# Moving a mixture-of-experts overflow branch into the expert loop, and three modulation chunks behind three projections

## The chip, the cores and the metric

The kernel runs on one core of a Trainium2 chip. The metric is the time of one execution on the device, in microseconds. The kernel before takes 1628.29 us (median of 3 runs, 1628.29 to 1628.72). The engines are TensorE (PE in the rows, its weight loads PEld), VectorE (DVE), ScalarE (ACT), GpSimd (POOL) and SyncE (SP); a letter q behind an engine's name stands for its sequencer, which takes branches, semaphores and the issue of transfers.

## The reference

Two layers over 256 latent and 256 context tokens of width 1024. Each layer normalises and modulates the tokens, projects them once, runs three token mixers (grouped-query attention, neighbourhood attention, an mLSTM scan) and merges them; then comes a mixture of experts. The modulation vectors come from a product with `w_mod` of each layer.

```
for l in range(DEPTH):                         # DEPTH = 2
    mod = silu(c) @ w_mod[l] + b_mod[l]        # and mod_c of the context vector: shifts, scales, gates
    h = modulate(rms_norm(x, g_norm[l, 0]), sh1, sc1)
    y, yc = token_mixers(h, hc, ...)           # h @ w_in, three branches, merge
    x = x + gt1 * y
    h = modulate(rms_norm(x, g_norm[l, 1]), sh2, sc2)
    x = x + gt2 * hier_moe(h, ...)
    # in layer 0 the same for the context tokens xc

def hier_moe(t):                               # top-1 of 4 groups, top-2 of its 8 experts
    for e in range(32):
        gu = t @ w_gate_up[e]
        y = (silu(gu[:, :256]) * gu[:, 256:]) @ w_down[e]
        out = out + dense_w[:, e:e+1] * y      # dense_w is 0 for the experts not chosen
```

In layer 0 the mixture of experts runs over 512 tokens (two halves of 256), in layer 1 over the 256 latent tokens.

## The kernel before

The tokens stand transposed, features on the 128 partitions, as eight tiles of 128 features (`KT` = 8). The kernel is recorded as straight code for five engines; a scheduler that plans over a time line orders the instructions of each engine, but it moves none across the edge of a block. A branch (`tc.If`) begins and ends a block, so nothing recorded behind it can be put ahead of it.

**The experts (`moe`).** Each expert has room for 32 tokens (`CAP`) of a half. The loop `for q in range(NQ)` takes four experts at a time, eight times. `gather` collects the tokens of experts by matmuls with one-hot matrices (L1270), `gate_up(q)` does the first product (L1309), `swiglu` the activation, `act_T(q)` turns the result (L1329), `down` does the second product (L1344), and `combine(q)` scatters the rows back by matmuls (L1234) and adds them to the tokens with VectorE (L1239). TensorE runs `gate_up(q)` ahead of `down(q-1)`. The weights come by SyncE, 1 MB to a transfer (L1026, `in_wgu` and `in_wdn`), into buffers that are free again when TensorE has used them; `fetch_up(l, q+2)` and `fetch_down(l, q+1)` issue them ahead.

**The overflow path (L1397 to L1453).** Behind the loop every engine loads the largest rank of a token within an expert (`mi`, TENSOR_LOAD of L1397) and compares it (L1399). Only if an expert has more than 32 tokens of a half, a loop over all experts computes the tokens left out; its weights come by SyncE into the `wraw` buffers. With these inputs the path is not taken: the trace has no instruction of its body. An engine that jumps the body first raises the semaphores that the body would have raised, and before it does, it waits for what it has under way itself; on SyncE these are its transfers. The branch stands once in each layer.

**The layer boundary.** Ahead of the branch in layer 0 stand the first weight of layer 1's projections (`prep(T["win"][1, 12])`) and two modulation chunks. `mod_chunk` multiplies 256 columns of `w_mod` (L238), turns the result (L243) and adds the bias. Behind the branch `mixers(1)` issues three `w_mod` transfers into `y` buffers (`held`, L707). The first projection (`pre_w`, of tokens scaled by their gain only, L370 and L371, in two parts h0 and l0) doesn't need the norm of the tokens; it is scaled afterwards (L700). Then come six modulation chunks (the three held ones and those of `mod_fill(2)`), the projections `win[13]`, `win[10]`, `win[11]`, and `winp`. Those need the normalised tokens: L286 and L301 on TensorE, L290, L323, L330 and L380 on VectorE. Each projection's weights are split into a high and a low part by ScalarE (L221) and VectorE (L222), and each product is three matmuls (L334, L335, L336).

Of the kernel before, what the change touches and what calls it, by code (L numbers as in the profile page):

```python
# [10 lines left out]
F32 = mybir.dt.float32  # L11
# [34 lines left out]
def tile_backbone(ctx: ExitStack, tc: tile.TileContext, T, out):  # L46
# [310 lines left out]
    def mixers(l, need_ctx, xsrc, stats):  # L357
# [351 lines left out]
        for c in range(2):  # L709
            if c < len(pre_w):  # L710
                proj_f(pre_w[c], N, lambda i, p: use_k(2 * c + i, p, True), h0, l0)
                for m, w in held:
                    mod_chunk(*m, pat, w)
                if held:
                    mod_fill(2)
                held = []
            else:
                proj_f(win[12 + c], N, lambda i, p: use_k(2 * c + i, p, False))
        for c in range(2):
            proj_f(win[10 + c], nq, lambda i, p: nc.scalar.copy(qTM[:, 2 * c + i, :nq], p))  # L720
        for f in shares:
# [398 lines left out]
    def moe(l, nt, st, rt):  # L1120
# [227 lines left out]


# [12 lines left out]
        for q in range(NQ):  # L1362
# [4 lines left out]
            if q > 0:  # L1367
                aT = act_T(q - 1)
# [11 lines left out]
            if o < 3:  # L1380
# [4 lines left out]
                if q % 2 == 1:  # L1385
                    xe = xe_next
        down(NQ - 1, act_T(NQ - 1))
        combine(NQ - 1)
        if l == 0:
            lead.append((prep(T["win"][1, 12]), norm_scale(1, 0, slice(0, KT))))  # L1390
            for _ in range(2):
# [4 lines left out]

        top = nc.values_load(mi[0:1, 0:1], min_val=0, max_val=2048,  # L1397
                             skip_runtime_bounds_check_because="the key is 1024 + a rank below 512, or a rank")
        with tc.If(top >= 1024 + CAP):  # L1399
            over = t2([512])[:, :ntt * 32].rearrange("p (t e) -> p t e", e=32)  # L1400
            nc.vector.tensor_scalar(over, key, float(1024 + CAP), None, op0=ALU.is_ge)
            nc.vector.tensor_tensor(out=dw[:, :ntt], in0=dw[:, :ntt], in1=over, op=ALU.mult)
            ec = mt[:, 512:544]
            nc.vector.tensor_copy(ec, iota32)
            hT = Slabs([s8("mg", [4, N]) for _ in range(2)], 4)
            for t in range(ntt):
                for k in range(KT):
                    q = ptr()
                    c = slice(128 * k, 128 * k + 128)
                    nc.tensor.matmul(q[:, :128], lhsT=hth[t // 2][:, t % 2, c].bitcast(F32), rhs=ident, start=True, stop=False)  # L1410
                    nc.tensor.matmul(q[:, :128], lhsT=htl[t // 2][:, t % 2, c].bitcast(F32), rhs=ident, start=False, stop=True)
                    nc.vector.tensor_scalar(
                        hT[k][:, 128 * t:128 * t + 128], q[:, :128], modT[l][:, 24 + k, t // 2:t // 2 + 1], None, op0=ALU.add)
            with tc.For_i(0, NQ, 1) as q4:
                for e in range(4):
                    g0, g1 = (wraw(
                        T["wgu"][l, bass.ds(q4, 1), 4 * hf:4 * hf + 4, :, e].rearrange("o k p n -> p (o k) n"), [4, 512])
                        for hf in range(2))
                    w0 = wraw(T["wdn"][l, bass.ds(q4, 1), :, :, :, e].rearrange("o c k p n -> p (o c k) n"), [4, 512])
                    wq = small([32])  # L1420
                    nc.vector.tensor_scalar(wq, ec, 0.0, 0.5, op0=ALU.is_equal, op1=ALU.mult)
                    nc.vector.tensor_scalar(ec, ec, -1.0, None, op0=ALU.add)
                    pickd = t2([512])[:, :ntt * 32].rearrange("p (t e) -> p t e", e=32)
                    nc.vector.tensor_tensor(
                        out=pickd, in0=dw[:, :ntt], in1=wq.unsqueeze(1).to_broadcast([128, ntt, 32]), op=ALU.mult)
                    wt = small([ntt])
# [147 lines left out]
```

## Time and profile before

| | |
|---|---|
| median of the runs | 1628.29 us (1628.29 to 1628.72) |
| the profiled execution, its span | 1630.45 us, 1628.7 us |
| TensorE | 1520.8 us busy, 93% |
| weight loads of TensorE | 1055.9 us, beside it |
| VectorE, ScalarE, GpSimd | 777.7, 593.2, 168.8 us |
| read from HBM | 344.33 MB, 213 GB/s over the span |
| expert loop of layer 0, from gate_up(0) to the last output matmul | 709.1 to 969.9 us |
| pause of SyncE's issues at the layer boundary | 947.43 to 976.56 us |
| expert loop of layer 1 | 1413.4 to the end |

The page's share of TensorE is a mean over stages with different limits; where the change acts, windows and timelines of single engines are read. Idle time of an engine is followed by what ended it, in brackets. [...]

### The profile page before, as it was taken

The numbers are of one execution on the slowest core, as the hardware profiler recorded it, in microseconds if no ns is written. First come the engines' busy times: TensorE is split into PE (matmuls) and PEld (weight loads), VectorE is DVE, ScalarE is ACT, GpSimd is POOL, SyncE is SP. The second block draws the span as 40 slices with busy tenths as digits, with TensorE's granted clock in tenths as the row PEclk, the third lists the DMA queues.
The fourth block names the chain that finished last, engine by engine and source line by source line (L and its number), as shares of the span: only waits on it lengthen the run. The fifth ranks groups of instructions, "written<-read, shape, count | busy, mean of one in ns | idle before, by whom it ended". The sixth has DMA issues, their size and how long they took to land. (4 is left out here: it accounts for less than half of the span.)

```text
span 1628.7 us, 26090 instructions
## 1 busy us (share of the span) xinstructions
PE 1520.8 (93%) x10713; PEld 1055.9 (65%) x10713; DVE 777.7 (48%) x1754; ACT 593.2 (36%) x1195; POOL 168.8 (10%) x154
## 2 busy tenths in 40 slices
PE   5999999999999999979999978999999999797776
PEld 3688789767767678844434435989978789632221
DVE  4637953543345425253334357378556556431222
ACT  4325642443343333432122135346355455311110
POOL 2200320100021003000000002003011112000000
PEclk9999999999999999989999998999999999898898
DMA  8552234323322154258999968642225448699998
GB/s 305 183 176 83 104 111 156 116 70 114 134 98 84 40 176 152 80 219 350 405 385 413 390 267 312 208 137 78 91 104 169 149 146 324 251 417 417 416 418 328
DMA packets 57200, 349.27 MB, mean 214 GB/s; under 512 B 6912, under 2 KB 8032, under 8 KB 20336
## 3 DMA queue, kind: packets, MB, share of 16 engines
q1 hardware_dynamic: 54720, 341.02, 54.7%
q10 hardware_dynamic: 1616, 5.24, 0.8%
q0 software_dynamic: 736, 1.24, 0.4%
q8 instruction: 88, 1.44, 0.4%
q14 instruction: 40, 0.33, 0.1%
HBM read 344.33 MB, written 3.15 MB: 213 GB/s over the span
## 5 line engine op out<-in xcount | busy, mean ns | idle before, releaser
L222 DVE TENSOR_TENSOR wlo<-wraw,whi 128x1024 fp32r<-128x1024 f32 (+1 forms) x152 | 191.6, 1262 | 173.4 <-ACT whi L221 157.4
L334 PE MATMUL mm<-h,whi 128*128 128x512 f32 (+1 forms) x656 | 227.1, 348 | 0.5 <-ACT whi L221 0.5
L335 PE MATMUL mm<-h,whi 128*128 128x512 f32 (+1 forms) x656 | 223.4, 342 | 0.0
L336 PE MATMUL mm<-h,wlo 128*128 128x512 f32 (+1 forms) x656 | 222.4, 343 | 0.1
L221 ACT CAST whi<-wraw 128x1024 fp32r<-128x1024 f32 (+1 forms) x152 | 155.5, 1026 | 170.7 <-PE mm L335 68.1
L334 PE MATMUL mm<-whi,h 128*128 128x256 f32 (+1 forms) x640 | 183.0, 289 | 0.0
L336 PE MATMUL mm<-whi,h 128*128 128x256 f32 (+1 forms) x640 | 182.8, 288 | 0.0
L335 PE MATMUL mm<-wlo,h 128*128 128x256 f32 (+1 forms) x640 | 182.2, 286 | 0.0
L334 PEld LDWEIGHTS mm<-h,whi 128*128 128x128 f32 x656 | 123.8, 189 | 35.7 <-issue 17.5
L336 PEld LDWEIGHTS mm<-h,wlo 128*128 128x128 f32 x656 | 123.4, 189 | 23.3 <-issue 10.1
L335 PEld LDWEIGHTS mm<-h,whi 128*128 128x128 f32 x656 | 124.2, 190 | 17.0 <-issue 5.3
L334 PEld LDWEIGHTS mm<-whi,h 128*128 128x128 f32 x640 | 121.5, 191 | 6.6 <-issue 4.0
L335 PEld LDWEIGHTS mm<-wlo,h 128*128 128x128 f32 x640 | 122.1, 191 | 1.0 <-DVE G L775 0.5
L336 PEld LDWEIGHTS mm<-whi,h 128*128 128x128 f32 x640 | 121.6, 191 | 1.5 <-issue 1.4
L1309 PE MATMUL at<-qkv,y 128*32 128x512 f32 x792 | 104.9, 615 | 8.1 <-DMA qkv<-in_wgu 8.0
L1239 DVE SCALAR_TENSOR_TENSOR qkv<-mm,c_modT,qkv 128x256 f32<-128x256 f32 x192 | 80.5, 477 | 38.6 <-PE mm L1234 38.6
L619 DVE TENSOR_REDUCE nmx<-at 128x1 f32<-128x512 f32 (+1 forms) x96 | 56.7, 599 | 54.7 <-PE at L605 53.9
L1309 PE MATMUL at<-wraw,y 128*32 128x512 f32 x552 | 74.5, 625 | 8.9 <-DMA wraw<-in_wgu 8.9
L537 POOL TENSOR_TENSOR s1p<-s1p,c_powm 128x8 f32<-128x8 f32 (+1 forms) x24 | 43.4, 1807 | 315.5 <-DVE s1p L535 114.0
L1317 DVE SCALAR_TENSOR_TENSOR a<-a,at 128x256 f32<-128x256 f32 x24 | 10.1, 421 | 136.8 <-ACT a L1316 136.8
L1275 ACT ACTIVATE y<-mm,c_modT 128x256 f32<-128x256 f32 x96 | 40.2, 471 | 94.0 <-PE mm L1270 91.7
L1316 ACT ACTIVATE a<-at 128x256 f32<-128x256 f32 x24 | 9.2, 384 | 178.5 <-PE at L1309 178.0
(378 smaller groups left out, 2586.9 us busy)
## 6 DMA issues: line engine op xcount, KB each, us to landing
qkv<-in_wgu SPq DMA_DIRECT2D x62, 1024.0 KB, 11.8
wraw<-in_win SPq DMA_DIRECT2D x56, 1024.0 KB, 4.8
wraw<-in_wgu SPq DMA_DIRECT2D x42, 1024.0 KB, 11.6
wraw<-in_wmod SPq DMA_DIRECT2D x39, 1024.0 KB, 4.9
qkv<-in_wdn SPq DMA_DIRECT2D x31, 1024.0 KB, 9.6
wraw<-in_wdn SPq DMA_DIRECT2D x19, 1024.0 KB, 11.8
h<-in_wgu SPq DMA_DIRECT2D x14, 1024.0 KB, 17.5
wraw<-in_wbr SPq DMA_DIRECT2D x24, 512.0 KB, 3.3
```

Source lines behind the costliest of these rows:

```text
L221: nc.scalar.copy(hv, src)
L222: nc.vector.tensor_sub(lv, src, hv.bitcast(F32))
L334: nc.tensor.matmul(out_, lhsT=lh, rhs=rh, start=first, stop=False)
L335: nc.tensor.matmul(out_, lhsT=lh, rhs=rl, start=False, stop=False)
L336: nc.tensor.matmul(out_, lhsT=ll, rhs=rh, start=False, stop=last)
L537: nc.gpsimd.tensor_tensor(out=r, in0=v, in1=powm[:, :2 * H], op=ALU.pow)
L619: nc.vector.tensor_reduce(nmx[:, hf:hf + 1], S[hf], axis=AX.X, op=ALU.max, negate=True)
L1239: nc.vector.scalar_tensor_tensor(xT[f][:, c], p[:, c], modT[l][:, 40 + f, v_:v_ + 1], xT[f][:, c], op0=ALU.mult, op1=ALU.add)
L1275: nc.scalar.activation(xe[:, k], p[:, 256 * (k % 2):256 * (k % 2) + 256], AF.Identity, bias=modT[l][:, 24 + k, v_:v_ + 1])
L1309: nc.tensor.matmul(gps[v_][CAP * e:CAP * e + CAP], lhsT=xe[v_][:, k, s0:s0 + CAP], rhs=w[e], start=(k == 0), stop=(k == KT - 1))
L1316: nc.scalar.activation(th[:, 0:256], gp[:, 0:256], AF.Tanh, bias=0.0, scale=0.5)
L1317: nc.vector.scalar_tensor_tensor(th[:, 0:256], th[:, 0:256], 1.0, gp[:, 0:256], op0=ALU.add, op1=ALU.mult)
```

## The change

Three things are changed.

- In `moe` the overflow path becomes a function, `overflow()`, called once in each layer's loop behind `q == 0`, with `act_T(0)` ahead of it. It thus stands ahead of `gate_up(1)`, `down(0)` and `combine(0)`.
- Its body takes its weights by GpSimd's queue into tiles of the `a2` pool, one 128 x 512 piece for each product, and turns the tokens anew for each expert. The statistics that it computed anew at its end are gone, since the tokens are complete only after the loop.
- In `mixers(1)` the three held chunks and `mod_fill(2)` stand behind `win[13]`, `win[10]` and `win[11]`.

```
             if c < len(pre_w):
                 proj_f(pre_w[c], N, lambda i, p: use_k(2 * c + i, p, True), h0, l0)
-                for m, w in held:
-                    mod_chunk(*m, pat, w)
-                if held:
-                    mod_fill(2)
-                held = []
             else:
                 proj_f(win[12 + c], N, lambda i, p: use_k(2 * c + i, p, False))
         for c in range(2):
             proj_f(win[10 + c], nq, lambda i, p: nc.scalar.copy(qTM[:, 2 * c + i, :nq], p))
+        for m, w in held:
+            mod_chunk(*m, pat, w)
+        mod_fill(2 if held else 0)
...
+        def overflow():
+            top = nc.values_load(mi[0:1, 0:1], min_val=0, max_val=2048, ...)
+            with tc.If(top >= 1024 + CAP):
...
+                def weights(src):
+                    w = a2([512])
+                    nc.gpsimd.dma_start(w, src.rearrange("o p n -> p (o n)"))
+                    return w
+                with tc.For_i(0, NQ, 1) as q4:
...
             if q > 0:
-                aT = act_T(q - 1)
+                if q > 1:
+                    aT = act_T(q - 1)
                 gps = [pat() for _ in range(ns)]
                 gate_up(q, xe, gps)
...
                 if q % 2 == 1:
                     xe = xe_next
+            if q == 0:
+                aT = act_T(0)
+                overflow()
         down(NQ - 1, act_T(NQ - 1))
         combine(NQ - 1)
...
-        top = nc.values_load(mi[0:1, 0:1], min_val=0, max_val=2048, ...)
-        with tc.If(top >= 1024 + CAP):
...
-                    g0, g1 = (wraw(T["wgu"][l, bass.ds(q4, 1), 4 * hf:4 * hf + 4, :, e]...) for hf in range(2))
-                    w0 = wraw(T["wdn"][l, bass.ds(q4, 1), :, :, :, e]...)
...
-            if nxt[0] is not None:
-                nxt[0].n = 0
-                for f in range(KT):
-                    nxt[0].step(xT[f])
-            else:
-                for f in range(0, KT, 2):
-                    emit(f)
```

What the scheduler makes of it, at three places. The first is TensorE in layer 0's loop, before: the last gathers (L1270), the turning of the activated rows of the first four experts (L1329) and their successors' first product (L1309, on the weights `qkv_6084` and on).

```order
2973 L1270 MATMUL mm_6495<-whi_6413,h_6175 128x256
2974 L1270 MATMUL mm_6495<-whi_6413,h_6176 128x256
2975 L1329 MATMUL tr_6506<-c_ident,a_1144_6418 128x128 x2
2976 L1309 MATMUL at_6513<-qkv_6084,y_6246 32x512
2977 L1329 MATMUL tr_6506<-c_ident,a_1145_6422 128x128 x2
2978 L1309 MATMUL at_6513<-qkv_6084,y_6246 32x512 x3
2979 L1309 MATMUL at_6514<-qkv_6084,y_6247 32x512 x4
2980 L1309 MATMUL at_6513<-qkv_6086,y_6246 32x512 x4
```

And with the change, up to the branch (its lines are now L1268, L1327 and L1307; L1349 and L1351 are the load and the compare; L1289 is a helper product for the next scatter):

```order
2975 L1268 MATMUL mm_6495<-whi_6413,h_6176 128x256
2976 L1327 MATMUL tr_6506<-c_ident,a_1144_6418 128x128 x2
2977 L1327 MATMUL tr_6506<-c_ident,a_1145_6422 128x128 x2
2978 L1289 MATMUL ao_8592<-rwT_6167,t_1853_8589 128x512
2979 L1349 TENSOR_LOAD mi_6173
2980 L1351 COMPARE_AND_BRANCH
```

The jump lands ahead of the first product of the next four experts:

```order
3642 L1363 UNCONDITIONAL_BRANCH
3643 L1351 UNCONDITIONAL_BRANCH
3644 L1307 MATMUL at_8389<-qkv_6084,y_6246 32x512 x4
3645 L1307 MATMUL at_8390<-qkv_6084,y_6247 32x512 x4
3646 L1307 MATMUL at_8389<-qkv_6086,y_6246 32x512 x4
```

Before, the first product began between the two halves of act_T(0); now both halves, a helper product and the branch stand ahead of it, and the body of the branch (672 matmuls in layer 0, 288 before) lies between.

The second place is SyncE at the layer boundary, before: the last two weights of the experts (`in_wdn`), the first weight of layer 1 (`in_win`), the branch, the three held transfers into `y` and those that follow it (the rows of the body lie between this piece and the next).

```order
191 L1026 DMA qkv_7916<-in_wdn 128x2048
192 L1026 DMA wraw_7918<-in_wdn 128x2048
193 L204 DMA wraw_8348<-in_win 128x2048
194 L1397 TENSOR_LOAD mi_6173
195 L1399 COMPARE_AND_BRANCH
```

SyncE behind the branch's body, before:

```order
226 L1399 UNCONDITIONAL_BRANCH x2
227 L707 DMA y_9218<-in_wmod 128x2048
228 L707 DMA y_9220<-in_wmod 128x2048
229 L707 DMA y_9222<-in_wmod 128x2048
230 L204 DMA wraw_9276<-in_wmod 128x2048
231 L204 DMA wraw_9338<-in_wmod 128x2048
232 L204 DMA wraw_9355<-in_wmod 128x2048
233 L204 DMA wraw_9372<-in_win 128x2048
```

SyncE with the change, at the same place:

```order
200 L1024 DMA qkv_9792<-in_wdn 128x2048
201 L707 DMA y_10430<-in_wmod 128x2048
202 L707 DMA y_10432<-in_wmod 128x2048
203 L1024 DMA wraw_9794<-in_wdn 128x2048
204 L204 DMA wraw_10224<-in_win 128x2048
205 L204 DMA wraw_10488<-in_wmod 128x2048
206 L707 DMA y_10434<-in_wmod 128x2048
207 L204 DMA wraw_10505<-in_win 128x2048
208 L204 DMA wraw_10567<-in_wmod 128x2048
209 L204 DMA wraw_10584<-in_win 128x2048
```

No branch stands there any more: two held transfers go ahead of the last `in_wdn`, the third follows closely, and the weight of `win[13]` (`wraw_10505`) is the third transfer behind the lead weight, with `wraw_10584` (of `win[10]`) two behind it.

The third place is VectorE at the layer boundary, before: the end of the sums of squares (L277), the branch, L371, and the normalised tokens from L323 on.

```order
1076 L277 TENSOR_TENSOR acc_8269<-acc_8269,a_1613_9053 128x512
1077 L277 TENSOR_TENSOR acc_8269<-acc_8269,a_1614_9056 128x512
1078 L1399 UNCONDITIONAL_BRANCH x2
1079 L290 TENSOR_SCALAR s1p_9110<-ao_9105 128x4
1080 L371 SCALAR_TENSOR_TENSOR qkv_9068<-qkv_5610,smp_8358,qkv_9066 128x256 x8
1081 L371 SCALAR_TENSOR_TENSOR qkv_9069<-qkv_5611,smp_8358,qkv_9067 128x256 x8
1082 L323 TENSOR_TENSOR a_1633_9148<-qkv_5610,acc_9119 128x512
1083 L323 TENSOR_TENSOR a_1637_9162<-qkv_5610,acc_9119 128x512
1084 L330 TENSOR_SCALAR t_1632_9147<-a_1633_9148,smp_8358,c_modT_129 128x256
1085 L330 TENSOR_SCALAR t_1634_9154<-a_1635_9155,smp_8358,c_modT_129 128x256
```

VectorE with the change, at the same place:

```order
1270 L371 SCALAR_TENSOR_TENSOR qkv_10281<-qkv_5611,smp_10234,qkv_10279 128x256 x4
1271 L408 TENSOR_REDUCE shb_10277<-at_10333 128x4
1272 L371 SCALAR_TENSOR_TENSOR qkv_10281<-qkv_5611,smp_10234,qkv_10279 128x256 x2
1273 L277 TENSOR_TENSOR acc_10145<-acc_10145,a_2103_10211 128x512
1274 L371 SCALAR_TENSOR_TENSOR qkv_10281<-qkv_5611,smp_10234,qkv_10279 128x256
1275 L222 TENSOR_TENSOR wlo_10508<-wraw_10505,whi_10507 128x1024
1276 L277 TENSOR_TENSOR acc_10145<-acc_10145,a_2105_10221 128x512
1277 L222 TENSOR_TENSOR wlo_10512<-wraw_10505,whi_10511 128x1024
1278 L290 TENSOR_SCALAR s1p_10322<-ao_10317 128x4
1279 L222 TENSOR_TENSOR wlo_10587<-wraw_10584,whi_10586 128x1024
1280 L323 TENSOR_TENSOR a_2136_10360<-qkv_5610,acc_10331 128x512
1281 L323 TENSOR_TENSOR a_2140_10374<-qkv_5610,acc_10331 128x512
```

The scaling L371 is now mixed with what stood ahead of the branch, and three splits L222 (`wlo_10508`, `wlo_10512`, `wlo_10587`: the weight of `win[13]` in two halves and the first half of that of `win[10]`) stand ahead of L323; before, they stood behind L380.

## Rows read from the trace of the kernel before

**Rows 1.** windows: length, busy PE PEld DVE ACT POOL, clock, DMA share, GB/s

```profile
736.00:744.00 8.00, 8.00 (x78) 2.50 (x80) 0.00 (x0) 0.59 (x1) 0.00 (x0) 1.00 0.66 225
...
776.00:964.00 188.00, 184.79 (x1532) 78.77 (x1525) 74.80 (x179) 37.47 (x78) 0.00 (x0) 1.00 0.97 401
...
1416.00:1610.00 194.00, 155.03 (x949) 50.19 (x943) 46.60 (x114) 23.83 (x54) 0.00 (x0) 0.91 1.01 417
```

**Rows 2.** timeline of TensorE, end of layer 0: start, length, line, [idle before]

```profile
966.11 3.83 PE L1234 MATMUL mm<-wlo,mg 128*128 128x256 f32 x24
...
980.04 1.87 PE L286 MATMUL ao<-c_ones,acc 128*128 128x1 f32 x8 [10.11 <-DVEq L1399]
...
1010.16 0.50 PE L334 MATMUL mm<-h,whi 128*128 128x512 f32 x1 [0.51 <-ACT whi L221]
...
1035.95 1.07 PE L238 MATMUL mm<-wraw,c_cpad 128*32 128x256 f32 x16
...
1036.95 0.39 PE L334 MATMUL mm<-whi,h 128*128 128x272 f32 x1
```

**Rows 3.** the overflow branch's line: ns min/median/max, first and last start

```profile
L1399 SPq EVENT_SEMAPHORE  x8: 17/17/17, 959.2 to 964.5; - x8
...
L1399 DVEq COMPARE_BRANCH  x1: 72/72/72, 979.4 to 979.4; - x1
...
L1399 PEldq COMPARE_BRANCH  x2: 3370/3422/3473, 969.8 to 1621.9; - x2
```

**Rows 4.** timeline of SyncE, transfers issued, end of layer 0

```profile
947.43 0.33 SPq L204 DMA_DIRECT2D wraw<-in_win  x1
...
976.56 1.28 SPq L707 DMA_DIRECT2D y<-in_wmod  x3
```

**Rows 5.** timeline of VectorE, end of layer 0

```profile
963.88 1.66 DVE L1239 SCALAR_TENSOR_TENSOR qkv<-mm,c_modT,qkv 128x256 f32<-128x256 f32 x4 [2.09 <-PE mm L1234]
...
969.06 1.22 DVE L222 TENSOR_TENSOR wlo<-wraw,whi 128x1024 fp32r<-128x1024 f32 x1
...
973.68 0.68 DVE L277 TENSOR_TENSOR acc<-acc,a 128x512 f32<-128x512 f32 x1
...
982.35 6.43 DVE L371 SCALAR_TENSOR_TENSOR qkv<-qkv,smp,qkv 128x256 fp32r<-128x256 f32 x16 [0.24 <-ACT qkv L370]
...
988.70 1.29 DVE L323 TENSOR_TENSOR a<-qkv,acc 128x512 f32<-128x512 f32 x2
...
995.14 1.28 DVE L380 TENSOR_TENSOR h<-t,h 128x512 fp32r<-128x512 f32 x2
```

**Rows 6.** page: one group of instructions and DMA issues (us to landing)

```profile
L221 ACT CAST whi<-wraw 128x1024 fp32r<-128x1024 f32 (+1 forms) x152 | 155.5, 1026 | 170.7 <-PE mm L335 68.1
...
qkv<-in_wgu SPq DMA_DIRECT2D x62, 1024.0 KB, 11.8
...
wraw<-in_win SPq DMA_DIRECT2D x56, 1024.0 KB, 4.8
```

**Rows 7.** windows as in Rows 1, where the clock falls and where not

```profile
24.00:28.00 4.00, 1.07 (x16) 0.50 (x16) 3.52 (x10) 2.42 (x6) 0.00 (x0) 1.00 1.03 425
...
28.00:34.00 6.00, 5.46 (x20) 4.08 (x21) 3.55 (x10) 2.83 (x8) 0.00 (x0) 0.72 1.01 418
...
1004.00:1010.00 6.00, 4.69 (x40) 2.00 (x38) 2.27 (x16) 1.85 (x4) 2.26 (x8) 0.72 0.62 216
...
1484.00:1492.00 8.00, 5.06 (x35) 1.75 (x34) 3.04 (x6) 1.17 (x2) 0.00 (x0) 1.00 1.01 418
```

**Rows 8.** timeline of TensorE, gate_up(0) to gate_up(1) of layer 0

```profile
735.69 0.44 PE L1329 MATMUL tr<-c_ident,a 128*128 128x128 f32 x2
...
736.05 4.92 PE L1309 MATMUL at<-qkv,y 128*32 128x512 f32 x43
```

**Rows 9.** timeline of SyncE, layer 1's expert loop

```profile
1414.49 4.36 SPq L1026 DMA_DIRECT2D qkv<-in_wdn  x4
```

**Rows 10.** timeline of TensorE, layer 1's expert loop

```profile
1424.27 1.07 PE L1309 MATMUL at<-h,y 128*32 128x512 f32 x8
```

More of the change, by code (lines that the diff above doesn't have):

```diff
@@ L1394, in moe @@
                 mod_chunk(*mods.pop(0), pat, w)
-        top = nc.values_load(mi[0:1, 0:1], min_val=0, max_val=2048,
-                             skip_runtime_bounds_check_because="the key is 1024 + a rank below 512, or a rank")
-        with tc.If(top >= 1024 + CAP):
[L1400 to L1426, printed above, removed]
-                    nc.vector.tensor_reduce(wt, pickd, axis=AX.X, op=ALU.add)
-                    aT = s8("y", [2, 512])
-                    for t in range(ntt):
-                        gp = pat()
-                        for k in range(KT):
-                            nc.tensor.matmul(
-                                gp, lhsT=hT[k][:, 128 * t:128 * t + 128], rhs=(g0, g1)[k // 4][:, k % 4],
-                                start=(k == 0), stop=(k == KT - 1))
-                        th = t2([512])
-                        nc.scalar.activation(th[:, 0:256], gp[:, 0:256], AF.Tanh, bias=0.0, scale=0.5)
-                        nc.vector.scalar_tensor_tensor(
-                            th[:, 0:256], th[:, 0:256], 1.0, gp[:, 0:256], op0=ALU.add, op1=ALU.mult)
-                        nc.vector.scalar_tensor_tensor(
-                            th[:, 256:512], th[:, 0:256], wt[:, t:t + 1], gp[:, 256:512], op0=ALU.mult, op1=ALU.mult)
-                        q = ptr()
-                        for i in range(2):
-                            nc.tensor.transpose(q[:, 128 * i:128 * i + 128], th[:, 256 + 128 * i:384 + 128 * i], ident)
-                        nc.scalar.copy(aT[:, :, 128 * t:128 * t + 128], q[:, 0:256].rearrange("p (a b) -> p a b", a=2))
-                    for f in range(KT):
-                        p = pmm()
-                        for kk in range(2):
-                            nc.tensor.matmul(
-                                p[:, :nt], lhsT=w0[:, 2 * (f // 4) + kk, 128 * (f % 4):128 * (f % 4) + 128], rhs=aT[:, kk, :nt],
-                                start=(kk == 0), stop=(kk == 1))
-                        for v_ in range(nt // 256):
-                            c = slice(256 * v_, 256 * v_ + 256)
-                            nc.vector.scalar_tensor_tensor(
-                                xT[f][:, c], p[:, c], modT[l][:, 40 + f, v_:v_ + 1], xT[f][:, c], op0=ALU.mult, op1=ALU.add)
-            if nxt[0] is not None:
-                nxt[0].n = 0
-                for f in range(KT):
-                    nxt[0].step(xT[f])
-            else:
-                for f in range(0, KT, 2):
-                    emit(f)
```

52 lines of the change are left out of this document (added).

## The prediction

> **What bounds the kernel now.** I read the page first, then windows of busy time by stretch, then the timelines of single engines where a stretch is not full. TensorE is the busiest engine by far, but one share over the whole span says little. In layer 0's expert loop it is busy 184.79 of 188 us; the transfers there are nearly full too (0.97), yet where they dip (0.66 from 736 to 744) TensorE has all of its 8 us: they wait for it to release weight buffers. So layer 0's loop is bound by TensorE, and what stops TensorE there lengthens the program. Layer 1's loop is the other way round: DMA share 1.01, TensorE busy 155.03 of 194 us [rows 1].
>
> The large hole is where layer 0 ends. TensorE's last output matmuls run from 966.11 for 3.83 us, and the next start at 980.04 after 10.11 us of idleness [rows 2]. The rows of the overflow branch (L1399) tell who did what in it [rows 3]: SyncE raises its eight semaphores from 959.2 to 964.5, since it waits there for its own transfers; its issues pause from 947.43 to 976.56, until all engines are past [rows 4]. TensorE's compare-and-branch takes 3473 ns, VectorE's 72. VectorE reaches it last, at 979.4, and VectorE's branch is what TensorE waits for.
>
> **The layer boundary.** The moved branch frees SyncE and takes away the fence, so that the scaling of layer 1's tokens (L371) mixes with the last expert sums (L1239 before, L1237 now). How much that gives is VectorE's to say, since its work stays. From 963.88 it has, by the durations of its timeline [rows 5]: 16 sums at 0.42 us (6.7), 16 L371 at 0.40 (6.4), four splits L222 at 1.22 (4.9), four L277 at 0.7 (2.8), two L352 and small ones (1.8 together, as those between the rows). That is 22.6 us without a gap, so 986.5, where L371 ended at 988.78 before: at most 2.3 us come from here.
>
> Then the new order on VectorE costs something. The split of a second weight (wlo_10587) now stands ahead of L323, the first step of the normalised tokens. Its transfer (wraw_10584) waits for wlo_10512, which is ready at 986.5; landing takes 4.8 us as a median of such transfers, its ScalarE cast 1.03 [rows 6] and the split 1.22: 993.6, with issue and hand-overs some 994. L323 started at 988.70 [rows 5], so it is late by 5.3 us, and so is the first L380: 995.14 + 5.3 = 1000.4. The projection win[13] needs that tile. It started at 1010.16, because six modulation chunks stood ahead of it [rows 2]. Now three of them stand ahead, in the idle time before 1000; the other three, about 1.07 us each [rows 2], and four transposes L243 at an estimated 0.35 stand behind. From win[13]'s start to the projection winp it took 1036.95 - 1010.16 = 26.8 us [rows 2]; now it takes 26.8 + 3.2 + 1.4 = 31.4, so 1031.8. TensorE has little to do between about 991 and 1000, and places with little work bring its granted clock to the lower level: after 1.07 us of work in 24 to 28 the mean clock is 0.72 over 6 us, and again 0.72 from 1004 to 1010, which is 0.28 x 6 = 1.7 us lost each time; 5.06 us in 1484 to 1492 lost none [rows 7]. I add 1.7: 1033.5 against 1036.95, and 0.7 for L243s that now come after that point: a gain of **2.7 us**. Bounds: a gain of 6 if the clock stays up and wraw_10584 lands 2 us sooner, a loss of 4 if it takes the 11.8 us of the crowded wgu transfers [rows 6]. Two more 1 MB wmod transfers stand ahead of the last wdn weights; at 417 GB/s [rows 1] that is 5 us on their landing. It may hold TensorE by 1 or 2 us around 964, beside VectorE's chain, so I cost it at nothing, and at 2 if that chain is not the limit.
>
> **The branch in layer 0's expert loop.** It now stands between gate_up(0) with the next gathers and gate_up(1). Before, the transposes of act_T(0) ran up to 735.69, and gate_up(1) followed without a pause [rows 8]. Every engine takes the branch; by the built order nothing late is queued ahead of it on VectorE or ScalarE, and SyncE's next transfer waits for gate_up(1) in any case. On TensorE the cost of jumping the unused body is seen twice, 3473 and 3370 ns [rows 3]. The last matmuls ended at 969.94 and the jump at 969.8 + 3.47 = 973.3, so 3.4 us of idleness. The body that it jumps grows (288 to 672 matmuls), so I do not expect less. At its old place this lay beside VectorE's work; here that cover is gone: gate_up(1) is next, and the loop is TensorE's [rows 1]. An idle time of 3.4 us also exceeds the 2.9 that preceded the lower clock at 28 [rows 7]; I take 2.0 us for that, from 0 to twice 1.7. **+5.4 us**, bounds 3.4 and 6.8.
>
> [...]
>
> **The branch in layer 1's expert loop.** Same stall, other bound: TensorE has 39 us of slack in 194 [rows 1], so only what the stall does to the transfers counts. Ahead of the branch SyncE has issued four wdn transfers from 1414.49 on and two wgu [rows 9]: 6.3 MB or 15.1 us at 417 GB/s, so until about 1430.8. The next wait for gate_up(1), which began at 1424.27 [rows 10]; the stall, the slower clock and a few matmuls later buffers come free, at about 1430.7 to 1432.2. **+1.2 us** of empty queue, bounds 0 and the whole stall, 3.4.
>
> **The end of the program.** The second branch's TensorE part (1621.9 to 1625.3, [rows 3]) lay beside the output transfers: **-0.1 us**, bounds 0 and -0.5. Weights on GpSimd's queue cost nothing when the body isn't run; they only leave SyncE with no transfer to wait for.
>
> **Sum.** -2.7 + 5.4 + 1.2 - 0.1 = +3.8 us. The profiled execution took 1630.45 us, 2.2 above the median; the sum is a difference within it and stands on the median alike: 1628.29 + 3.8 = 1632.1, so **1632 us**.
>
> **Rivals.**
> *The boundary's hole goes for good.* SyncE's pause from 947.43 to 976.56 may have cost more than VectorE's list says. If the second weight does not hold L323 and no clock falls, win[13] starts at 995 and TensorE is full from there: 995 + 31.4 = 1026.4, which is 10.5 us. With the branches' 6.5 that is 1624.3: faster. For it speaks the 10.11 us hole, against it that VectorE ended the hole. It decides when the first L380 starts before about 997.
> *The stall is hidden after all.* If the jump costs TensorE the 0.1 us of the other engines, or queued matmuls run on beneath it, the two branches are worth about 0.5 us and the boundary's gain stays: 1626. Against it speak two rows of 3.4 us.
> *The jump is slower among transfers.* Both measured jumps were taken while transfers stood still or nearly so. The landing of 1 MB goes from 4.8 to 11.8 us where transfers are dense [rows 6]; if what the jump waits for is a transfer too, 3.4 becomes up to 8.4, in both loops: 1632 + 5 + 2 = 1639.
> [...]
> *The change does not do what it says* (the body is run, or a fence stays): the built order speaks against it, 0.01.
>
> **How the numbers follow.** The forecast gets 0.55, with a range of its own of 1629 to 1635; the boundary's rival 0.20, the hidden stall 0.14, the slower jump 0.10, the last 0.01. A difference under 0.2% (3.3 us, 1625.0 to 1631.55) is one that this measurement cannot tell from none. The forecast lies only 0.5 above that: I put 0.31 of its 0.55 slower, 0.24 the same. Slower is then 0.31 + 0.10 = 0.41. Faster is 0.17 of the first rival and 0.05 of the second; I raise it to 0.27, since VectorE's chain is a count of mine that may hide slack, which leaves 0.32 for the same. The range is 1622.5 to 1638: it takes in the first rival, and stops short of the full price of the slower jump.
>
> **What would show it.** The changed profile should have a compare-and-branch of some 3.4 us on TensorE near 735, a gap of that length before gate_up(1) and a clock below 1.00 soon behind it; empty transfers for about a microsecond near 1431 + 3; transfers without a long pause from 944 to 1000; L323 at about 994 and the projection winp at 1033.5, both plus the 5.4 us that layer 0 lost. I am wrong if gate_up(1) follows without a gap, if L323 starts before 990 (plus what layer 0 lost), or if the rest of layer 0's loop makes up for the gap.

## The result and the profile after

The changed kernel takes 1646.04 us (median of 4 runs, 1645.86 to 1649.29) against 1628.29; the ratio is 1.0109, with a 95% interval of [1.0097, 1.012]. It is slower by 17.8 us, where 3.8 were forecast and 1638 was the upper end of the range: the direction was right, the size was not. The profiled execution took 1645.86 us, with a span of 1644.0.

The branch first. These rows of the branch's line (now L1351) answer to [rows 3]: TensorE's compare-and-branch in layer 0 and in layer 1, in ns (min/median/max) and with its start.

```profile
L1351 PEldq COMPARE_BRANCH  x1: 3964/3964/3964, 735.8 to 735.8; - x1
...
L1351 PEldq COMPARE_BRANCH  x1: 5939/5939/5939, 1437.0 to 1437.0; - x1
```

TensorE's timeline around both (start, length, line, and in brackets the idle time before), to be read beside [rows 8, 10]:

```profile
735.14 0.47 PE L1289 MATMUL ao<-rwT,t 32*128 32x512 f32 x1
740.03 1.93 PE L1307 MATMUL at<-qkv,y 128*32 128x512 f32 x8 [4.42 <-DVE smp L314]
...
1436.56 0.38 PE L1292 MATMUL ao<-rwT,t 64*128 64x256 f32 x1 [0.21 <-DVE t L1290]
1443.23 1.94 PE L1307 MATMUL at<-h,y 128*32 128x512 f32 x8 [6.29 <-PEq L1351]
```

The gap before gate_up(1) is 4.42 us in layer 0 and 6.29 us in layer 1. The second bracket names the branch itself; the first names VectorE, but a jump that began at 735.8 and took 3.96 us ends at 739.8, so it is the jump there too, but for the last 0.2 us. The eight matmuls behind each gap take 1.93 us; the eight of [rows 10] took 1.07. The windows say why (length, busy time by engine, granted clock as a share of its highest, DMA share, GB/s):

```profile
740.00:744.00 4.00, 3.97 (x20) 1.12 (x24) 0.17 (x1) 0.00 (x0) 0.00 (x0) 0.50 0.03 6
744.00:748.00 4.00, 4.00 (x40) 1.29 (x36) 0.00 (x0) 0.00 (x0) 0.00 (x0) 0.93 0.75 285
...
1439.00:1443.00 4.00, 0.00 (x0) 0.00 (x0) 0.00 (x0) 0.00 (x0) 0.00 (x0) 0.74 0.98 401
1443.00:1447.00 4.00, 3.77 (x20) 1.22 (x24) 0.00 (x0) 0.00 (x0) 0.00 (x0) 0.50 0.27 78
```

In both loops the granted clock is 0.50 for 4 us behind the gap. In layer 0 that loses 2.3 us (2.0 and 0.28). In layer 1 the transfers were full (0.98) while TensorE jumped, and ran dry behind it (0.27 of the time, so 2.9 us).

At the layer boundary the 10.11 us hole of [rows 2] is gone, and smaller ones are in its place. TensorE from the last down product (L1342) on:

```profile
971.86 1.92 PE L1342 MATMUL mm<-wraw,kva 128*32 128x512 f32 x16
976.51 0.65 PE L1232 MATMUL mm<-wlo,mg 128*128 128x256 f32 x2 [2.72 <-ACT mg L351]
979.17 1.22 PE L1232 MATMUL mm<-wlo,mg 128*128 128x256 f32 x4 [2.02 <-DVE mg L352]
...
1009.42 1.22 PE L334 MATMUL mm<-h,whi 128*128 128x512 f32 x2 [5.34 <-ACT h L379]
1010.57 1.94 PE L238 MATMUL mm<-wraw,c_cpad 128*32 128x256 f32 x16
1014.56 0.80 PE L335 MATMUL mm<-h,whi 128*128 128x512 f32 x1 [2.06 <-DVE h L380]
...
1046.25 0.52 PE L334 MATMUL mm<-whi,h 128*128 128x272 f32 x2 [1.42 <-ACT whi L221]
```

The last expert sums wait 2.72 us for a split on ScalarE (L351) and 2.02 us for its other half on VectorE (L352). ScalarE's timeline shows what stood ahead of the split:

```profile
974.56 0.51 ACT L370 ACTIVATE qkv<-qkv,smp 128x256 fp32r<-128x256 f32 x1 [0.50 <-DVE qkv L1237]
...
974.97 0.61 ACT L273 ACTIVATE a<-qkv 128x512 f32<-128x512 f32 x1
975.49 0.49 ACT L370 ACTIVATE qkv<-qkv,smp 128x256 fp32r<-128x256 f32 x1
975.89 0.56 ACT L351 CAST mg<-mm 128x512 fp32r<-128x512 f32 x1
```

It is layer 1's scaling (L370), which itself waits for VectorE's sums. VectorE's timeline answers to [rows 5]:

```profile
985.73 3.23 DVE L1237 SCALAR_TENSOR_TENSOR qkv<-mm,c_modT,qkv 128x256 f32<-128x256 f32 x8 [3.75 <-PE mm L1232]
...
996.11 1.22 DVE L222 TENSOR_TENSOR wlo<-wraw,whi 128x1024 fp32r<-128x1024 f32 x1
...
1003.27 1.23 DVE L222 TENSOR_TENSOR wlo<-wraw,whi 128x1024 fp32r<-128x1024 f32 x1 [1.52 <-ACT whi L221]
1004.73 2.36 DVE L323 TENSOR_TENSOR a<-qkv,acc 128x512 f32<-128x512 f32 x2 [0.24 <-ACT acc L305]
...
1013.83 1.28 DVE L380 TENSOR_TENSOR h<-t,h 128x512 fp32r<-128x512 f32 x2
```

SyncE's timeline has this issue, to be read beside [rows 4]:

```profile
997.35 0.33 SPq L204 DMA_DIRECT2D wraw<-in_win  x1
```

The chain that was forecast is there: the split ends at 997.33, the transfer of win[10]'s weight is issued at 997.35, its split begins at 1003.27, and L323 follows it at 1004.73. But the first of these, forecast for 986.5 plus the 5.4 of layer 0, comes 10.8 us behind 986.5, and from L323 to L380 it takes 9.1 us instead of 6.4.

### The profile page after: what moved, and what is told of

It is laid out like the page before. It is cut to its first block, busy times and chain, and to the rows that moved or that the text cites. A ratio compares the mean times of both kernels' runs of the same rounds, so it can differ in the third digit from the quotient of the medians.

```text
span 1644.0 us, 26106 instructions
## 1 busy us (share of the span) xinstructions
PE 1525.0 (93%) x10713; PEld 1059.4 (64%) x10713; DVE 779.6 (47%) x1754; ACT 591.6 (36%) x1195; POOL 170.6 (10%) x154
## 5 line engine op out<-in xcount | busy, mean ns | idle before, releaser
L222 DVE TENSOR_TENSOR wlo<-wraw,whi 128x1024 fp32r<-128x1024 f32 (+1 forms) x152 | 190.5, 1255 | 166.9 <-ACT whi L221 156.2
L221 ACT CAST whi<-wraw 128x1024 fp32r<-128x1024 f32 (+1 forms) x152 | 155.4, 1026 | 179.2 <-PE mm L335 68.4
L1307 PE MATMUL at<-qkv,y 128*32 128x512 f32 x792 | 105.3, 626 | 17.3 <-DMA qkv<-in_wgu 12.7
L1307 PE MATMUL at<-wraw,y 128*32 128x512 f32 x552 | 73.8, 643 | 7.2 <-DMA wraw<-in_wgu 7.2
## 6 DMA issues: line engine op xcount, KB each, us to landing
wraw<-in_wdn SPq DMA_DIRECT2D x19, 1024.0 KB, 10.8
```

What stands on the lines that cost most here:

```text
L221: nc.scalar.copy(hv, src)
L222: nc.vector.tensor_sub(lv, src, hv.bitcast(F32))
L1307: nc.tensor.matmul(gps[v_][CAP * e:CAP * e + CAP], lhsT=xe[v_][:, k, s0:s0 + CAP], rhs=w[e], start=(k == 0), stop=(k == KT - 1))
```

## The experiments

Since the start of the program differs by up to 5 us from one execution to the next, places are given as microseconds behind the start of gate_up(0) of layer 0 in the same profile. All are read off TensorE's timeline, from one profile of each kernel; the last column but one is the median of the runs, the last the ratio to the kernel before with its interval. How far two profiles differ by themselves can be seen from the changed kernel and run 7, whose code is the same up to layer 1's loop: 1.3 us at winp, 2.6 at gate_up(0) of layer 1.

| kernel | gate_up(1) | last sums end | winp | layer 1: gate_up(0) | gate_up(1) | last matmul ends | us | ratio |
|---|---|---|---|---|---|---|---|---|
| before | 25.6 | 260.8 | 327.8 | 704.2 | 715.2 | 913.2 | 1628.3 | |
| changed | 31.6 | 278.0 | 337.8 | 716.3 | 734.8 | 930.7 | 1646.0 | 1.0109 [1.0097, 1.012] |
| 1 branch only | 31.5 | 278.0 | 339.5 | 716.7 | 735.3 | 931.0 | 1646.1 | 1.0115 [1.0098, 1.0133] |
| 2 chunks only | 25.6 | 261.0 | 329.3 | 706.6 | 717.5 | 916.3 | 1633.1 | 1.0026 [1.0012, 1.0039] |
| 3 no branch | 25.6 | 272.1 | 330.4 | 707.6 | 719.4 | 916.7 | 1631.4 | 1.0019 [1.001, 1.0029] |
| 4 no branch, old chunks | 25.6 | 273.5 | 332.1 | 709.1 | 720.0 | 918.6 | 1631.0 | 1.0013 [1.0003, 1.0023] |
| 5 short body | 25.8 | 271.3 | 329.4 | 706.8 | 718.6 | 916.4 | 1629.7 | 1.0012 [0.9999, 1.0025] |
| 6 expert loop | 31.4 | 277.9 | 337.0 | 714.3 | 732.9 | 929.4 | 1644.8 | 1.0098 [1.0083, 1.0112] |
| 7 short in layer 1 | 31.4 | 277.3 | 336.5 | 713.7 | 724.6 | 924.1 | 1639.4 | 1.006 [1.0042, 1.0079] |
| 8 scaling behind splits | 25.6 | 267.1 | 329.1 | 706.9 | 717.8 | 916.3 | 1630.1 | 0.9999 [0.9984, 1.0014] |
| 9 transfers behind lead | 25.6 | 261.0 | 326.9 | 704.2 | 715.1 | 913.3 | 1627.2 | 0.9998 [0.9987, 1.0008] |
| 10 tokens first | 25.6 | 260.9 | 325.4 | 703.4 | 714.3 | 912.7 | 1627.8 | 0.9995 [0.9982, 1.0008] |
| 11 end, GpSimd's queue | 25.6 | 265.9 | 331.4 | 708.7 | 719.9 | 918.2 | 1633.8 | 1.0023 [1.001, 1.0037] |
| 12 chunks ahead | 25.6 | 266.7 | 322.1 | 699.0 | 709.9 | 908.9 | 1628.4 | 1.0001 [0.9988, 1.0014] |
| 13 chunks ahead, behind lead | 25.6 | 260.9 | 322.8 | 699.8 | 711.6 | 909.8 | 1626.2 | 0.9984 [0.9974, 0.9994] |
| 14 end, loop, chunks | 25.6 | 260.9 | 327.1 | 703.8 | 715.0 | 912.8 | 1628.7 | 0.9993 [0.9983, 1.0003] |

**Which part of the change (1 to 4).** Run 1 is the changed kernel with the chunks where they were:

```
                 proj_f(pre_w[c], N, ...)
+                for m, w in held: mod_chunk(*m, pat, w)
+                if held: mod_fill(2)
+                held = []
-        for m, w in held: mod_chunk(*m, pat, w)
-        mod_fill(2 if held else 0)
```

> The branch moved into the expert loop as in the changed kernel, the modulation chunks left behind the first projection. Theory F (fence): the two branches cost 4.9 and 5.5 us, the end gives back 1.5, and the layer boundary loses about 5 us because without the fence of the old branch the scaling of layer 1's tokens (L370, L371) gets ahead of the splits L351 and L352 that the last expert sums need: 1640 to 1646 us, TensorE waiting over 2 us for ScalarE's L351 near 975. Rival C (chunks): the boundary loses because of the chunks' new place, so it is 1636 to 1638 here. Rival S (stalls alone): the boundary's loss follows from what the branch does upstream, and nothing changes against the changed kernel: 1646.

Run 2 moves the chunks, and nothing else, in the kernel before.

> The kernel before with only the six modulation chunks moved behind the projections win[13], win[10], win[11]; the branch stays at each layer's end. Theory F: the fence still holds the scaling back, so the boundary is as before but for the chunks, which now follow: 1625 to 1631 us. Rival C: the second weight's split ahead of L323 and the chunks behind cost the boundary its 5 us here as well: 1632 to 1635.

Run 3 is the changed kernel with `overflow()` not called (`- overflow()`).

> The changed kernel with the overflow path left out in both layers (it is not taken with these inputs; the branch itself is gone). Theory F: what is left is the boundary's loss without the two stalls: 1646 - 4.9 - 5.5 = 1635 to 1637 us, TensorE still waiting for L351 and L352 at the end of layer 0. Rival S: with the branches gone the boundary recovers too: 1624 to 1630.

Run 4 is run 3 with the chunks in their old place.

> The kernel before with the overflow path left out in both layers, so no fence, no stall and the chunks in their old place. Theory F: the mixing of L370 and L371 with the last sums comes with the missing fence, so this is not faster than the kernel before by the 10 us of its hole, but 1628 to 1636 us. Rival C: with chunks in the old place and no branch the hole is filled: 1616 to 1622. Rival S: 1618 to 1624.

The branch alone makes the whole loss (run 1), so the chunks' place (rival C) isn't its cause; alone under the old fence it costs 4.4 us by the runs (run 2). Without a branch 14.7 of the 17.8 us are gone (run 3 against the changed kernel). That is more than the 10.4 of theory F, and part of the boundary's loss goes with the branch, as rival S says: winp comes 7.4 us earlier (330.4 instead of 337.8), about 2 us more than the delay in the middle of the loop (5.6, below). The last sums are late without a fence in every one of runs 1, 3 and 4 (272 to 278, against 261 with it in run 2), as F says, whichever way the chunks stand. Filling the hole by taking the fence away gives nothing by itself.

**What in the branch (5, 6, 7).** Run 5 cuts the body behind its first three VectorE instructions, so that TensorE has no code left in it:

```
                 ec = mt[:, 512:544]
                 nc.vector.tensor_copy(ec, iota32)
-                def weights(src): ...
-                with tc.For_i(0, NQ, 1) as q4: ...
```

> The changed kernel with the branch in its new place, but its body cut to three VectorE instructions (the rest of the overflow path is left out; it is not run with these inputs anyway). Theory J (the jump over the long body is the price): TensorE's compare-and-branch falls from 3964 and 5939 ns to under 200 ns, gate_up(1) follows within 1.5 us and the time comes to 1631 to 1635 us, near the kernel without a branch. Rival B (the block's edge is the price: loads on every engine, no instruction moved across): the jump may be short, but the time stays at 1640 or more.

TensorE's compare-and-branch in it, layer 0 and layer 1:

```profile
L1351 PEldq COMPARE_BRANCH  x1: 228/228/228, 728.5 to 728.5; - x1
...
L1351 PEldq COMPARE_BRANCH  x1: 213/213/213, 1421.9 to 1421.9; - x1
```

16.3 us go with the long body, though none of it is ever run. What is left of the change, with the block's edge, the loads and the place, costs 1.2 us (1629.72 against 1628.47 of the kernel before, taken beside it), within the interval. Theory J holds, though the time is a little below its range; rival B falls.

Run 6 keeps the path whole, but loops over the four experts on the chip:

```
-                    for e in range(4):
+                    with tc.For_i(0, 4, 1) as e4:
+                        e = bass.ds(e4, 1)
```

> The changed kernel with the four experts of the body as a loop on the chip instead of four copies: TensorE's body is a quarter as long (168 matmuls in layer 0, 84 in layer 1), nothing else is changed and nothing is left out. Theory J (the jump over code that isn't held is the price, with a step and not in proportion): the shorter jump of layer 1 falls to 0.2 us as with the short body, that of layer 0 either stays at 3.4 to 4 us (1634 to 1638) or falls as well (1629 to 1632). Rival P (in proportion to the length): 1.0 and 1.5 us, 1632 to 1634. Rival N (any body with TensorE work costs the same): 4 and 6 us, 1644 to 1647.

TensorE's compare-and-branch in it, layer 0 and layer 1:

```profile
L1351 PEldq COMPARE_BRANCH  x1: 3748/3748/3748, 735.2 to 735.2; - x1
...
L1351 PEldq COMPARE_BRANCH  x1: 5979/5979/5979, 1434.5 to 1434.5; - x1
```

A quarter of the body costs as much as the whole, so the price isn't in proportion to the length: here rival N was right, and my expectation missed. That some code is held and some isn't, no run shows. The run settles another question. In the changed kernel VectorE stands still behind its branch too: its compare takes 0.07 us, but its next instruction follows 3.35 and 5.40 us later.

```profile
L1351 DVEq COMPARE_BRANCH  x2: 68/70/72, 736.3 to 1437.4; - x2
L1351 DVEq EVENT_SEMAPHORE  x2: 21/21/21, 739.7 to 1442.9; - x2
```

In run 6 that pause is 0.5 us, as in the kernel before, and gate_up(1) is as late as with the pause (31.4 against 31.6). So it is TensorE's own jump that delays it.

Run 7 is the changed kernel with the body cut as in run 5, but in layer 1 alone (`+ if l == 1: return` ahead of `weights`).

> The changed kernel with the body cut to three VectorE instructions in layer 1 alone (the rest of layer 1's overflow path is left out); layer 0 keeps its long body. Of the 16 us between the changed kernel and the one with both bodies short, theory J puts 7 to 8 us on layer 1's jump of 5.9 us with its clock, less the 2 us that the transfers' slack takes, so 5 to 6, and the rest, 10, on layer 0's jump and on the boundary behind it: 1639 to 1641 us. Rival: layer 1 is bound by transfers, so its jump costs only the 3 us in which they stand empty: 1642 to 1644.

With 1639.4, layer 1's jump is worth 6.7 us by the medians (1646.04 - 1639.36) and layer 0's, with what it does to the boundary, 9.6 (1639.36 - 1629.72). These shares are known to a microsecond or two: run 7's interval alone is 6 us wide. By the profiles layer 1's loop, from gate_up(0) to the last matmul, takes 214.3 to 215.1 us with the long jump (the changed kernel, runs 1 and 6) and 209.0 to 210.5 in all others, so 4 to 6.

**What goes with the jump.** The price of the jump is 3.37 and 3.47 us in [rows 3], 3.96 in layer 0 of the changed kernel, where the transfers stood still from its middle on, and 5.94 in layer 1 (5.98 in run 6), where they were full. The run with the branch at the layer's end (11, below) gives both in one kernel: full transfers at 970 (0.97 of the time from 970 to 972, 0.95 to 974), and 0.41 of the time during the jump at the end.

```profile
L1353 PEldq COMPARE_BRANCH  x1: 5833/5833/5833, 970.4 to 970.4; - x1
...
L1353 PEldq COMPARE_BRANCH  x1: 3598/3598/3598, 1623.5 to 1623.5; - x1
```

The profile's DMA view of the jump in layer 1 of the changed kernel (queue, kind: packets, MB, share of 16 engines) has one packet of 0.02 MB on an instruction queue beside the weights:

```profile
q1 hardware_dynamic: 329, 2.40, 97.1%
q8 instruction: 1, 0.02, 1.1%
q14 instruction: 3, 0.02, 1.0%
```

and of the jump at 969.8 in the kernel before nothing else:

```profile
q8 instruction: 1, 0.02, 1.9%
```

In the four microseconds from the short body's branch of layer 1 there is none:

```profile
q1 hardware_dynamic: 234, 1.67, 100.0%
```

Such packets also come where nothing jumps (88 on this queue in the changed kernel, one in 19 us), so one beside a jump isn't proof by itself. What says more is when it comes. Narrower windows of the same view place it: in the kernel before, 1 us behind the start of the jump at 969.8; in layer 1 of the changed kernel there is none from 1437 to 1440, and then one.

```profile
q8 instruction: 1, 0.02, 6.8%
...
q8 instruction: 1, 0.02, 2.2%
```

The first of these is the view of 970.8 to 971.8 before, the second that of 1440 to 1443 with the change. It is so in every profile here. In each of the 18 jumps that took over 3 us, exactly one packet of that queue begins, and the jump ends 2.3 to 2.7 us behind its start. In the thirteen that took 3.4 to 4.0 us it begins 0.9 to 1.5 us behind the jump's start (transfers 0.01 to 0.49 of the time); in the five that took 5.8 to 7.0 us, with full transfers at their start, 3.3 to 4.7. In the four jumps under 0.4 us none begins.

So each long jump goes with one packet of that queue, and among full transfers it is the packet's beginning that comes late, by 2 to 4 us. The step with the body's presence is shown by experiment (0.23 and 0.21 us against 3.96 and 5.94); that the jump waits for the packet is read from 18 jumps that end at the same distance from it, and no run held the packet back alone.

**What takes the place of the hole (8 to 10).** These start from run 3, with the overflow path left out. Run 8 queues each L370 and L371 behind the last splits:

```
-                    nc.scalar.activation(h0[k][:, c], ...)
+                    with tc.issue_after(last_split[0].ins) if l == 1 else nullcontext():
+                        nc.scalar.activation(h0[k][:, c], ...)       # L371 likewise on VectorE
```

> The changed kernel without the overflow path (as in the run without a branch) and with each L370 and L371 of layer 1 queued behind the last splits L351 and L352 of the expert loop, on its engine. Theory F: the last expert sums on TensorE end 11 us earlier than in the run without a branch (near 967 where gate_up(0) starts at 706), VectorE's L323 starts earlier, and the time falls by 3 to 8 us below that run's 1631.4: 1623 to 1628. Rival V (VectorE's amount of work is the limit, not its order): L323 and the projections come no earlier, 1630 to 1633.

Run 9 also issues the three held transfers behind the last expert weight and the lead weight (`+ with tc.issue_after(lead_dma.ins):` around `nc.sync.dma_start`).

> The changed kernel without the overflow path (left out in both layers), with L370 and L371 behind the last splits as in an earlier run, and the three held wmod transfers behind the last expert weight and the first weight of layer 1. Theory T (transfers): in the earlier run the last down product ended 2.6 us late, since two wmod transfers stood ahead of its weights; here it ends as early as before (257.1 us after gate_up(0) starts), the last sums follow, and winp starts 2 to 3 us earlier against gate_up(0) than the 329.1 us of that run: 326 to 327.5, time 1626 to 1629. Rival V (VectorE's work is the limit): winp no earlier than 328.5, 1629 to 1632.

Run 10 also puts L221 of win[10] and win[11] behind L379 on ScalarE, and their L222 and L700 behind L380 on VectorE (`+ with tc.issue_after(last_shift[1].ins):`).

> As the run before this one, and ScalarE and VectorE do the normalised tokens (up to L380) ahead of the splits of win[10] (L221, L222) and of the scaled first projection (L700). Theory O (order): L380 starts 5 to 8 us earlier against gate_up(0) than in the run without a branch (298.3 us there, 286.0 in the kernel before), and winp starts at 321 to 325 us after gate_up(0) (327.9 in the kernel before): 1621 to 1626. Rival V: VectorE does the same work in another order, what is put behind comes late instead, and winp stays at 327 to 330: 1628 to 1632.

By the profiles winp comes at 330.4, 329.1, 326.9 and 325.4 with no, one, two and three of the orders mended: 1.3, 2.2 and 1.5 us each, about as much as two profiles can differ, but 5.0 together, and with all three 2.4 us ahead of the kernel before. The last sums move with the first two orders: 272.1, 267.1, 261.0. Run 9 is at theory T's mark; run 8 gained less than F's 3 to 8, run 10 less than O's. Rival V, that the amount of VectorE's work is the limit, falls for these 5 us at winp, though run 8's time lies in its range. The medians go from 1631.4 to 1630.1, 1627.2 and 1627.8, but the last three intervals overlap one another and 1.

**Other places for the branch and the chunks (11 to 14).** Run 11 keeps the branch at the layer's end and takes the new body:

```
                 mod_chunk(*mods.pop(0), pat, w)
+        overflow()      # with the statistics computed anew at its end
```

> The kernel before with the overflow path at the end of each layer, as it was, but with the new body whose weights come by GpSimd's queue; chunks in the old place. Theory: SyncE no longer waits for transfers (no eight semaphores from 959 to 964), but its next transfers still stand behind the branch; VectorE ends TensorE's hole as before, so the gain is 0 to 3 us: 1625 to 1629. TensorE's jump takes 3.4 to 6 us and lies in the hole. Rival: SyncE's pause was the limit, the held weights arrive about 10 us earlier and the chunks run without waits: 1620 to 1624.

It is slower by 0.2% (interval [1.001, 1.0037]), against the expectation. SyncE no longer waits, its transfers are full at 970, and TensorE's jump takes 5.83 us. L286 comes at 274.4 instead of 270.9, but the jump had ended at 976.3, 3.9 us before it; the row names VectorE's branch.

```profile
980.15 1.86 PE L286 MATMUL ao<-c_ones,acc 128*128 128x1 f32 x8 [8.47 <-DVEq L1353]
```

VectorE reached the branch at 977.16 and went on 2.85 us behind it (0.51 in the kernel before, with the shorter body), and the last sums had ended 5.1 us later (265.9 against 260.8).

Run 12 records five chunks ahead of the old branch, with the body unchanged:

```
+            for _ in range(3):
+                w = s8("y", [KT, 256])
+                nc.sync.dma_start(w, T["wmod"][mods[0]])
+                mod_chunk(*mods.pop(0), pat, w)
+            mod_fill(2, pat)
```

> The kernel before with five of the modulation chunks (three into y, two of the fill) recorded ahead of the branch at layer 0's end, so that they fall into TensorE's hole; the overflow path unchanged. Theory H (the hole is room): some 8 us of TensorE's work move from 997 to 1010 into 970 to 980, win[13] starts 5 to 9 us earlier: 1620 to 1625 us. Rival V: VectorE ends the hole, and win[13] needs L380, which started at 995 and ended at 1003; the gain is 2 to 5 us: 1624 to 1627. Rival W: SyncE waits longest for its own transfers, of which there are now more ahead of the branch, and the hole grows: 1629 to 1633.

Run 13 issues their transfers behind the lead weight (`+ with tc.issue_after(last_dma[0].ins):`).

> The kernel before with five modulation chunks ahead of layer 0's last branch, as in the earlier run, but their transfers behind the last expert weight and the first weight of layer 1, so that they hold up neither. Theory H: the last down product is no longer late (966 where gate_up(0) starts at 709, against 970 in the earlier run), and the program is 2 to 5 us faster than with the chunks alone: 1622 to 1626 us. Rival W: SyncE now waits at the branch for transfers that land near 975, the fence opens later, and nothing is gained: 1627 to 1631.

Run 14 joins runs 11, 6 and 13.

> The branch at each layer's end with the weights on GpSimd's queue, the body's experts as a loop, and the five chunks ahead of the branch with their transfers behind the first weight of layer 1. Nothing is left out. If theory J and theory H hold, SyncE does not wait, TensorE's jump is short or lies beside VectorE, and the chunks fill the hole: 1618 to 1624 us. If the fence is opened by VectorE and not by SyncE or TensorE, no better than the run before this one: 1622 to 1628.

In the profiles of runs 12 and 13 winp comes 5 to 6 us sooner and the last matmul ends 3.5 to 4.4 sooner: the hole was room. By the runs only 13 is faster than the kernel before, 1626.24 against 1629.26 taken beside it (0.9984, [0.9974, 0.9994]); for 12 the interval takes in both. Why run 12's profile is so much better than its median stays open. In run 14 SyncE's transfers of win[13] go ahead of the branch, since no SyncE instruction is in its body, so the edge of a block holds them less than I had written. TensorE's jump meets full transfers: half of the engines' time goes to SyncE's weights, the other half to ScalarE's transfers of the tokens (`xs`).

```profile
q10 hardware_dynamic: 194, 1.47, 50.3%
q1 hardware_dynamic: 201, 1.38, 49.8%
```

It takes 7.0 us, the longest seen, TensorE's next matmul waits 7.3 us for it, and the time is above both ranges expected. But it takes 0.36 at the program's end, though the same loop is jumped:

```profile
L1343 PEldq COMPARE_BRANCH  x1: 6996/6996/6996, 983.8 to 983.8; - x1
...
L1343 PEldq COMPARE_BRANCH  x1: 363/363/363, 1622.2 to 1622.2; - x1
```

In that short jump no packet of queue 8 begins. So whether such a packet comes at all isn't set by the body alone; what else sets it, no run shows.

## Why the prediction was wrong

Measured on one scale, from gate_up(0) of layer 0 in the two profiles, the forecast's terms came out so: layer 0's loop +5.6 (forecast +5.4), the boundary up to winp +4.4 (forecast -2.7), from there to layer 1's loop +2.0 (not in the sum, and hardly more than two profiles differ), layer 1's loop +5.5 (forecast +1.2), the end -1.5 (forecast -0.1). That is 16.0 of the 17.8; the rest is the scatter of single executions. So the boundary and layer 1's loop are the steps that failed.

*The branch in layer 0's loop, +5.4: right in the loop, not behind it.* Gap and clock came as described: gate_up(1) is 6.0 us late, the first down product 7.7 (39.9 to 47.6 behind gate_up(0)), by the gap of 4.42, its clock (2.3) and the turned rows that no longer overlap with it. The loop then gives 2 back: gate_up(5) begins at 860.52 before and at 865.41 with the change, 151.4 and 157.0 behind gate_up(0).

```profile
860.52 1.92 PE L1309 MATMUL at<-qkv,y 128*32 128x512 f32 x16
865.41 1.92 PE L1307 MATMUL at<-qkv,y 128*32 128x512 f32 x16
```

That the loop came so near to 5.4 is luck in part: the jump took 3.96 us and not 3.4 (3.83 in run 2 with the transfers still, so the traffic need not be the reason), and the new order of the loop is worth 1.1 us by itself (150.3 in run 5). Against run 5 the jump costs 6.7 us there, 8.4 at winp (7.1 in run 7), and 9.6 by the medians; why the delay grows at the boundary stays open.

*The branch in layer 1's loop, +1.2: mis-sized.* It costs 5.5 us by the profiles (214.5 against 209.0 from gate_up(0) to the last matmul) and 6.7 by the medians of run 7. The stall was taken as 3.4 us, the price in quiet; among full transfers it was 5.94, and gate_up(1) came 7.6 us later than the offset at gate_up(0) (19.6 against 12.0). The 6.3 MB counted ahead of it did run out, and the transfers stood nearly still for 2.9 us. The third rival had named the place ("among transfers") and a wait for a transfer, with 8.4 us as its price and 0.10 as its chance; the place is shown, the wait is read from the 18 jumps above. Its chance was too low: I took the quiet price as the likely one, though the place of the change was the crowded one. Its reading that both jumps before fell on still transfers was wrong for the second, which had them 0.43 of the time (from 1621.9 to 1625.3); that this made it no longer says little for full ones, as the packet of queue 8 came before most of them, 1.0 us behind the jump's start.

*The layer boundary, -2.7: wrong in sign.* With short jumps it is +1.6 us at winp (run 5), though the loop ahead of it is 1.1 us faster. The bound of VectorE's list, 22.6 us without a gap, did not hold: from the first sum at 969.47 to the end of wlo_10512 at 997.33 it took 27.9 us, 24.1 of work and one gap of 3.75, in which VectorE waited for the last sums on TensorE (L1232), and those for splits that stood behind L370 and L371. I had said that TensorE's sums were early enough to be hidden beside VectorE, and had not asked what ScalarE and VectorE do ahead of the splits that feed them. "It may hold TensorE by 1 or 2 us ... I cost it at nothing" was wrong too: mending the order of transfers is worth 6.2 us at the last sums and 2.2 at winp (run 9 against run 8). With all three orders mended the boundary gains 2.4 us, about what I had put down for the kernel as it was built. The delay of L323 by win[10]'s weight was right. The 0.35 us of a transpose L243 was an estimate of mine from no row; in the trace before, the median of 96 is 0.27. In the kernel before, SyncE's pause ended ahead of the last engine's branch: it issued again at 976.56, and VectorE came to its compare at 979.4 [rows 3, 4].

*The end, -0.1:* it gave back 1.5 us. From the last matmul to the end of the span it was 6.3 us (1622.4 to 1628.7) and is 4.8 (1639.2 to 1644.0).

*Rivals.* The hidden stall fell by the first row. The boundary's rival, that the hole goes for good, fell as built; runs 12 and 13 come nearest to it, by filling the hole, not by removing it. By the medians the terms are 9.64 + 6.68 + 1.43 = 17.75, where 1.43 is run 5 against the kernel before and holds the boundary and the end; this sum closes by the way it is made, since each term is the difference of two neighbouring medians.

## What to carry to other kernels

Price a branch that is never taken on every engine that has code in its body (here 3.4 to 7.0 us on TensorE, once 0.36, against 0.21 to 0.23 without), and by the transfers that run meanwhile (3.4 to 4.0 us with up to half of their time, 5.8 to 7.0 among full ones): here a hole of 10.11 us beside VectorE's work was a good place for it, and the middle of the expert loops a bad one, 16.3 us by run 5. Before a fence is taken away, list on every engine what will move ahead of the work that others wait for, for the order that the fence kept by accident may be worth as much as its hole (here the last sums ended 11.3 us later without it, at 272.1 against 260.8); if a hole can't be closed, put independent work into it.

## What was not expected of the hardware

A compare-and-branch on TensorE took 0.21 to 0.23 us over a body without TensorE's code and, once, 0.36 over a long one at the program's end; 3.4 to 4.0 us over a long body where transfers had up to half of the time; and 5.8 to 7.0 us where it began among full ones. It ended 2.3 to 2.7 us behind the start of one packet on an instruction queue, each of 18 times. A body of a quarter of the length cost TensorE the same (3.75 and 5.98 us against 3.96 and 5.94), while VectorE's pause behind its own compare fell from 3.35 and 5.40 us to 0.5.
